# Token-major output projections, norms and residual stream with transposes back to feature-major

## The chip, the cores and the metric

The kernel runs on one core of one Trainium2 chip. A core has TensorE (PE: matmuls into PSUM), ScalarE (ACT), VectorE (DVE), GpSimd (POOL), SyncE (SP, which here issues most DMAs) and 16 DMA engines. The metric is device time in microseconds. The time before is 2262.39 us, the median of 3 runs (2261.51 to 2263.01).

## What is computed

Two layers of a diffusion backbone over 512 latent tokens and 256 context tokens, 1024 features, fp32. Layer 0 mixes tokens by retention (4 heads), layer 1 by HGRN2 (8 heads); each is followed by a gated convolutional FFN with 2816 hidden features. Cut to what the change touches:

```
mod = silu(c) @ ada_w[i] + ada_b[i]          # shift, scale, gate for each of two halves of a layer
u_l = rms_norm(h_l, norm_g[i, 0]) * (1.0 + sc1_l) + sh1_l
y_c, y_l = mixer(u_c, u_l, ...)              # ends in  (...) @ w_out
h_l = h_l + g1_l * rms_norm(y_l, norm_g[i, 1])
u_l = rms_norm(h_l, norm_g[i, 2]) * (1.0 + sc2_l) + sh2_l
h_l = h_l + g2_l * rms_norm(conv_ffn(u_l, ..., w_down), norm_g[i, 3])
# the same for the context stream with c_ctx, in layer 0 alone
```

The RMS norms go over the 1024 features of a token. The gain of a norm of y is the gate g times norm_g, one number per feature and per stream (latent or context).

## The kernel before

Activations lie feature-major: 128 features on the partitions, tokens along the free dimension, 8 feature tiles. Each matmul in fp32 precision is three in fp32r: every operand is split into a rounded part hi and a rest lo (`split`, L55: ScalarE writes hi, VectorE or GpSimd lo), and hi x hi, hi x lo, lo x hi are summed in PSUM. `weights` (L67) loads a weight block by a DMA on SP and splits it; raw, hi and lo have two buffers each. PSUM has six banks for large results (`acc`, L43) and two for small ones (`sml`, L46).

The order of PE's instructions is that of the program (`run`, L1200, puts PE under a manual schedule). The other engines' queues are ordered by the scheduler from a model of the timeline, except ScalarE in a part of `tail` (L444) and in the first stage.

The stages are `retention` (L582), `ffn` of layer 0 (L874), `hgrn` (L970) and `ffn` of layer 1, each ending in `tail` (L396), which also starts the next one. The output projection is done in parts while the stage still runs: for retention three heads of four (L844 to L858), for the FFN 18 of 22 hidden tiles in `down` (L919), for HGRN four heads of eight in `out1` (L1137). In these, weights are the stationary operand and tokens stream: one output tile is 128 features by 512 latent tokens and, in layer 0, 128 features by 256 context tokens. `evac` (L387) puts the sum into y in SBUF, by a copy on ScalarE the first time and by an add on VectorE after that.

`tail` does the last four k tiles in chunks of 256 tokens (three chunks with context, else two), 8 feature tiles each, 12 matmuls of 256 columns per tile (L401). For every chunk a generator `post` (L299) then does: load the residual h of the chunk by a DMA, squares of y on ScalarE and their pairwise sums on VectorE, the gain on ScalarE (L331), the sum over features by matmuls with a matrix of ones (`colsum`, L92, fp32), the root (`rstd`, L96: one on ScalarE, three refining steps on VectorE, each 256 wide on all partitions), the multiplication of y (L340, VectorE), the residual add (L343, mostly GpSimd), the store of h (L348, GpSimd's queue), the same norm for h, the multiplication (L355), modulation by A and B (`modulate`, L383, GpSimd) and the split into u (L368). `tail` calls the generators in pieces between the matmuls, and `lead` (L462) does the first four output tiles of the next stage, chunk by chunk, with the rest of the generators as hooks. In the last tail each quarter of a chunk is stored to the output (L345).

The modulation vectors come from `ada` (L200): pieces of work that fillers run between other matmuls; `finish` (L231) puts a section into feature-major form by a matmul with a selection table, and `modvec` (L276) multiplies it with the norm's weight.

Of the kernel before, what the change touches and what calls it, by code (L numbers as in the profile page):

```python
# [32 lines left out]
class Net:  # L33
# [70 lines left out]
    def setup(self):  # L104
        nc, cp = self.nc, self.cp
        cT = self.const("cT", eng=nc.sync)
        self.fold, self.ada_b, self.norm_g, self.sel = (self.const(c) for c in ("fold", "ada_b", "norm_g", "sel"))
        self.ones = cp.tile([P, P], F32, name="ones")
# [9 lines left out]
        self.mv = {}  # L118
        self.fill, self.acc_due, self.fin_due = deque(), None, None
# [80 lines left out]
    def ada(self, i, s, spread=False):  # L200
# [30 lines left out]
        def finish():  # L231
            n = 16 if spread else 64
            g = self.cp.tile([64, P], F32, tag="arow", name=f"arow{i}_{s}")[:n]
            nc.scalar.dma_start(g, scr.rearrange("j v (f c) -> (j v f) c", c=P))
            pt = self.sml(f"adat{i}_{s}", 16)
# [40 lines left out]
    def modvec(self, i, which):  # L276
# [3 lines left out]
        j, s = {"A1": (0, 1), "G1": (1, 2), "A2": (2, 4), "G2": (3, 5)}[which]  # L280
        gb = self.norm_g[:, i, j].unsqueeze(2).broadcast_to([P, NF, 2])
        o = self.cp.tile([P, NF, 2], F32, name=f"mv{i}{which}")
        if which[0] == "A":
            nc.vector.scalar_tensor_tensor(o, m[:, s], 1.0, gb, ALU.add, ALU.mult)
        else:
            nc.vector.tensor_tensor(o, m[:, s], gb, ALU.mult)
# [12 lines left out]
    def post(self, nm, chunk, y, hsrc, G, mods, u, hdst, big, tmp, early=False, fast=False, late=None):  # L299
# [4 lines left out]

        def squares(parts, kind):
            for p, a in enumerate(parts):
                q = pair(sums, p // 2) if p % 2 == 0 else tmp(f"q{kind}{p}{nm}").rearrange("p (a t) -> p a t", a=2)
                nc.scalar.activation(q, a, AF.Square)  # L308
                if p % 2:
                    nc.vector.tensor_tensor(pair(sums, p // 2), pair(sums, p // 2), q, ALU.add)  # L310

        def norm(kind):
            ps = self.sml(f"nps{kind}{nm}", W)
            if y is None:
                nc.vector.tensor_tensor(pair(sums, 0), pair(sums, 0), pair(sums, 1), ALU.add)
            self.colsum(ps, [sums[:, j] for j in range(2 if y is None else 4)])
            r = tmp(f"r{kind}{nm}")
            return self.rstd(r[:, :W], r[:, W:], ps, D)

        hx = big([P, NF + 4, W], F32, "hc" + nm)  # L320
        if early:
            yield "new"
# [3 lines left out]
        if y is not None:  # L326
# [19 lines left out]
            if u is None:  # L346
                return
# [957 lines left out]
```

## Time and profile before

| | |
|---|---|
| median of 3 runs | 2262.39 us (2261.51 to 2263.01) |
| the profiled execution's own time | 2261.59 us |
| its span in the profile | 2259.9 us |
| mean granted clock | 0.979 |
| PE busy | 2149.8 us (95%), 13144 matmuls |
| VectorE, ScalarE, GpSimd busy | 1403.3, 835.0, 429.5 us |
| DMA | 215.09 MB, mean 95 GB/s |

How to read it: a line of the page's groups gives the kernel line, engine, operation, the tiles written and read, shapes and count, then busy time and mean ns of one, then idle time of the engine before these instructions and what ended it. A row of a tile gives minimum, median and maximum duration, and the first and last start. In rows of time, the first number is the start in us from the span's start, the second how long the merged instructions took. The granted clock is that of TensorE, 1.00 being full speed. Matmuls are pipelined, so the duration of one is longer than the distance to the next.

### The profile page before, as it was taken

The numbers are of one execution on the slowest core, as the hardware profiler recorded it, in microseconds if no ns is written. First come the engines' busy times: TensorE is split into PE (matmuls) and PEld (weight loads), VectorE is DVE, ScalarE is ACT, GpSimd is POOL, SyncE is SP. The second block draws the span as 40 slices with busy tenths as digits, with TensorE's granted clock in tenths as the row PEclk, the third lists the DMA queues.
The fourth block names the chain that finished last, engine by engine and source line by source line (L and its number), as shares of the span: only waits on it lengthen the run. The fifth ranks groups of instructions, "written<-read, shape, count | busy, mean of one in ns | idle before, by whom it ended". The sixth has DMA issues, their size and how long they took to land. (4 is left out here: it accounts for less than half of the span.)

```text
span 2259.9 us, 32506 instructions
## 1 busy us (share of the span) xinstructions
PE 2149.8 (95%) x13144; PEld 1843.6 (82%) x13144; DVE 1403.3 (62%) x2546; ACT 835.0 (37%) x1575; POOL 429.5 (19%) x481
## 2 busy tenths in 40 slices
PE   7999999999899799999999979999999889999997
PEld 5888888888788788888888878888888668888886
DVE  6866675744515667467676577677777756434445
ACT  5542433423424333322132254434443444333323
POOL 4522130400102500000000055333333231000001
PEclk9999999999999899999999989999999999999998
DMA  8123213133123133333333422111111242232341
GB/s 284 57 67 124 81 57 125 53 122 113 56 73 119 63 112 104 122 112 117 108 112 127 154 75 85 57 39 57 39 57 42 91 150 87 92 104 94 102 135 43
DMA packets 204822, 215.09 MB, mean 95 GB/s; under 512 B 5760, under 2 KB 192512, under 8 KB 203904
## 3 DMA queue, kind: packets, MB, share of 16 engines
q1 hardware_dynamic: 199968, 198.90, 27.4%
q0 software_dynamic: 2608, 13.11, 1.7%
q8 instruction: 103, 1.69, 0.3%
q10 hardware_dynamic: 2096, 1.01, 0.2%
q14 instruction: 47, 0.39, 0.1%
HBM read 197.69 MB, written 15.31 MB: 94 GB/s over the span
## 5 line engine op out<-in xcount | busy, mean ns | idle before, releaser
L84 PE MATMUL f<-um,hua 128*128 128x512 f32 (+1 forms) x960 | 257.9, 356 | 0.0
L84 PE MATMUL f<-um,huv 128*128 128x512 f32 (+1 forms) x960 | 255.8, 354 | 0.0
L219 DVE SCALAR_TENSOR_TENSOR rows<-rada,sc,rows 128x256 f32<-128x256 f32 x504 | 232.2, 485 | 5.2
L84 PE MATMUL f<-gt,hd 128*128 128x512 f32 (+1 forms) x864 | 233.1, 358 | 0.0
L343 POOL TENSOR_TENSOR hce<-hce,yf 128x512 f32<-128x512 f32 x16 | 24.7, 1567 | 904.7 <-PE tl L407 538.5
L84 PEld LDWEIGHTS f<-um,hua 128*128 128x128 f32 x960 | 169.7, 189 | 28.5 <-issue 3.2
L84 PE MATMUL hp<-ue,hhw 128*128 128x512 f32 (+1 forms) x672 | 192.1, 373 | 0.0
L84 PEld LDWEIGHTS f<-um,huv 128*128 128x128 f32 x960 | 170.1, 189 | 25.2
L84 PEld LDWEIGHTS f<-gt,hd 128*128 128x128 f32 x864 | 152.4, 188 | 26.8 <-issue 0.6
L84 PE MATMUL f<-um,lua 128*128 128x512 f32 (+1 forms) x480 | 170.1, 354 | 0.0
L84 PE MATMUL f<-um,luv 128*128 128x512 f32 (+1 forms) x480 | 169.7, 354 | 0.0
L84 PE MATMUL f<-gt,ld 128*128 128x512 f32 (+1 forms) x432 | 154.4, 357 | 0.0
L84 PEld LDWEIGHTS hp<-ue,hhw 128*128 128x128 f32 x672 | 111.9, 189 | 17.7 <-issue 1.4
L676 PE MATMUL v<-hv,ua 128*128 128x512 f32 x384 | 120.5, 390 | 0.0
L84 PE MATMUL hp<-ue,lhw 128*128 128x512 f32 (+1 forms) x336 | 120.0, 357 | 0.0
L84 PEld LDWEIGHTS f<-um,lua 128*128 128x128 f32 x480 | 90.7, 189 | 13.0
L84 PEld LDWEIGHTS f<-um,luv 128*128 128x128 f32 x480 | 90.7, 189 | 12.6
L904 DVE TENSOR_TENSOR c<-f,c 128x512 f32<-128x512 f32 (+1 forms) x60 | 36.1, 601 | 100.7 <-PE f L84 100.6
L84 PEld LDWEIGHTS f<-gt,ld 128*128 128x128 f32 x432 | 81.2, 188 | 13.2
L891 ACT ACTIVATE c<-f,c_conv_b,c_conv_w 128x512 f32<-128x512 f32 (+1 forms) x60 | 41.9, 702 | 118.1 <-PE f L84 118.1
L84 PE MATMUL ld<-um,hfl 128*128 128x256 f32 x320 | 69.2, 313 | 17.1 <-ACT um L56 10.0
L1072 POOL TENSOR_SCALAR L<-Q 128x256 f32<-128x256 f32 x112 | 54.9, 505 | 160.9 <-PE hl L1085 63.0
(388 smaller groups left out, 5215.7 us busy)
## 6 DMA issues: line engine op xcount, KB each, us to landing
rada<-ada_w SPq DMA_DIRECT2D x48, 1024.0 KB
rua<-ffn_w_up SPq DMA_DIRECT2D x20, 1024.0 KB
ruv<-ffn_w_up SPq DMA_DIRECT2D x20, 1024.0 KB
rd<-ffn_w_down SPq DMA_DIRECT2D x24, 768.0 KB
rhw<-hg_w_in SPq DMA_DIRECT2D x32, 512.0 KB
rv<-ret_w_in SPq DMA_DIRECT2D x8, 1024.0 KB
rg<-ret_w_in SPq DMA_DIRECT2D x8, 1024.0 KB
rqk<-ret_w_in SPq DMA_DIRECT2D x6, 1024.0 KB
```

The lines of the kernel that those rows point to most:

```text
L84: nc.tensor.matmul(o, a, b[:, s], start=(i == 0), stop=(i == n - 1))
L219: nc.vector.scalar_tensor_tensor(rows[:, v], raw[:, k], a, rows[:, v], ALU.mult, ALU.add)
L343: eng.tensor_tensor(pair(hc, p), pair(hc, p), pair(y[p // 2][:, :, cs], p % 2), ALU.add)
L676: nc.tensor.matmul(ps, a, b, start=(c == 0 and k == 0 and z == 0), stop=(c == 1 and k == 3 and z == 2))
L891: nc.scalar.activation(c[:, s], ps, AF.Identity, bias=cb[:, i, mt : mt + 1], scale=w(1))
L904: nc.vector.tensor_tensor(c[:, s], ps, c[:, s], ALU.mult)
L1072: nc.gpsimd.tensor_scalar(vw(L[:, 1])[:, :, hf[1 - d]], vw(Q[:, d])[:, :, hf[1 - d]], 1.0, 0.0, ALU.mult, ALU.add)
```

## The change

The projections turn round: activations are now the stationary operand and the weights stream, so that an output tile is 128 tokens by 512 features; y and h lie token-major in blocks of 128 tokens (six blocks with context, four without). Each norm's sum over features is then along the free dimension and comes from the squares' accumulator output on ScalarE; the root and its refining steps work on one column. The gain, which is now along the free dimension, is a table of rows in DRAM (`gain_rows`), broadcast to all partitions by a DMA on ScalarE's queue. Once a block's unit-norm h is there, eight PE transposes of 128 x 128 bring it back to feature-major in PSUM, and ScalarE applies modulation while it evicts them, one feature tile at a time; the splits into u follow. GpSimd keeps only the stores of h and the lo part of some weights. `post` stays, as `norm_in`, for the first stage alone. The inputs gain a token-major copy of h and small tables; the output is token-major.

In the tail two column halves of a block follow one another; `n0` pairs run their first three k tiles ahead of the last. Transposes of the first blocks come between matmuls of the tail, the others as hooks in the lead. The weights of the projection loops are loaded in blocks of 512 columns (retention: six loads of 4 k tiles; down: four loads per part, of 3 k tiles). The DMA scratch of GpSimd's queue is set to 4096.

```diff
+    def gain_rows(self, i, s, g, n):
+        nc = self.nc
+        tab = self.cp.tile([16, 2, P], F32, tag="gtab", name=f"gtab{i}_{s}")
+        nc.scalar.dma_start(tab, self.t["gain_tab"][i, s // 5])
+        ps = self.sml(f"adag{i}_{s}", P)[0:16]
+        nc.tensor.matmul(ps, self.rsel[:n], g, start=True, stop=True)
+        nc.vector.tensor_tensor(tab[:, 0], ps, tab[:, 0], ALU.add)
+        nc.vector.scalar_tensor_tensor(tab[:, 0], tab[:, 0], -0.5 / D, tab[:, 1], ALU.mult, ALU.mult)
+        nc.scalar.dma_start(self.gains[i, s].rearrange("v (f c) -> (v f) c", c=P), tab[:, 0])
...
+    def handover(self, nm, y, hsrc, gain, mods, u, hdst, nb, big, tmp):
+        nc = self.nc
+        per = y[0].shape[1]
+        hx = [big([P, 3, D], F32, f"hx{nm}{j}") for j in range((nb + 2) // 3)]
+        if nb % 3:
+            g = hx[-1][:, 2:3]
+        else:
+            g = big([P, 3, D], F32, "gr" + nm)[:, 0:2]
+        small = lambda n, w: self.cp.tile([P, w], F32, tag=f"sm{w}", name=f"{n}{nm}", bufs=6)
+
+        def load():
+            rows = hsrc.rearrange("(b p) d -> p b d", p=P)
+            for j, x in enumerate(hx):
+                n = min(3, nb - 3 * j)
+                nc.sync.dma_start(x[:, :n], rows[:, 3 * j : 3 * j + n])
+            for v in range(g.shape[1]):
+                nc.scalar.dma_start(g[:, v], self.gains[gain][v : v + 1].broadcast_to([P, D]))
+
+        def block(b):
+            ts, v = slice(b * P, b * P + P), int(b >= 4)
+            yb, hb = y[b // per][:, b % per], hx[b // 3][:, b % 3]
+            ss = small(f"ss{b}", 4)
+            r = small(f"r{b}", 2)
+            for c in range(2):
+                cs = slice(c * 512, c * 512 + 512)
+                ps = yield
+                nc.vector.tensor_tensor(yb[:, cs], ps, yb[:, cs], ALU.add)
+                nc.scalar.activation(tmp(f"sq{nm}{b}{c}"), yb[:, cs], AF.Square, accum_out=ss[:, c : c + 1])
+            nc.vector.tensor_tensor(ss[:, 2:3], ss[:, 0:1], ss[:, 1:2], ALU.add)
+            ry = self.rstd(r[:, 0:1], r[:, 1:2], ss[:, 2:3], D)
+            nc.vector.scalar_tensor_tensor(yb, yb, ry, g[:, v], ALU.mult, ALU.mult)
+            nc.vector.tensor_tensor(hb, hb, yb, ALU.add)
+            if u is None:
+                nc.sync.dma_start(hdst[ts], hb)
+                yield "end"
+                return
+            nc.gpsimd.dma_start(hdst[ts], hb)
+            nc.scalar.activation(yb, hb, AF.Square, accum_out=ss[:, 3:4])
+            r2 = small(f"q{b}", 2)
+            rh = self.rstd(r2[:, 0:1], r2[:, 1:2], ss[:, 3:4], D)
+            nc.scalar.activation(yb, hb, AF.Copy, scale=rh)
+            yield "z"
+            A, B = mods()
+            z = yb.rearrange("p (f c) -> p f c", c=P)
+            for j in range(2):
+                ps = self.sml(f"tr{nm}{b}{j}")
+                for f in range(4):
+                    nc.tensor.transpose(ps[:, f * P : f * P + P], z[:, 4 * j + f], self.ident)
+                for f in range(4):
+                    k = 4 * j + f
+                    nc.scalar.activation(z[:, k], ps[:, f * P : f * P + P], AF.Identity,
+                                         scale=A[:, k, v : v + 1], bias=B[:, k, v : v + 1])
+                self.split(u[j][:, :, ts], u[2 + j][:, :, ts], z[:, 4 * j : 4 * j + 4])
+            yield "u"
+
+        return load, [block(b) for b in range(nb)]
 
...
+    def evac(self, y, b, c, ps, first):
+        per = y[0].shape[1]
+        dst = y[b // per][:, b % per, c * 512 : c * 512 + 512]
+        if first:
+            self.nc.scalar.activation(dst, ps, AF.Copy)
+        else:
+            self.nc.vector.tensor_tensor(dst, ps, dst, ALU.add)
+
+    def tail(self, w, x, y, nb, mk, nxt, mid=None):
+        load, gens = mk(nb)
+        load()
+        for g in gens:
+            next(g)
+
+        def part(b, c, kr, ps):
             for k in kr:
+                xh, xl = (z[:, b * P : b * P + P] for z in x(k))
+                for z, (l, r) in enumerate(((xh, w[c][0]), (xh, w[c][1]), (xl, w[c][0]))):
+                    self.nc.tensor.matmul(ps, l, r[:, k], start=(k == 0 and z == 0), stop=(k == 3 and z == 2))
+            if kr[-1] == 3:
+                gens[b].send(ps)
+
+        order = [(b, c) for b in range(nb - 2) for c in range(2)] + [(nb - 2 + b, c) for c in range(2) for b in range(2)]
+        n0 = 2 if mid is None else 4
+        pss = [self.acc(f"tl{self.uid()}") for _ in range(n0)]
+        for e, ps in zip(order, pss):
+            part(*e, range(3), ps)
+        if mid is not None:
+            self.filler(mid)
+        for e, ps in zip(order, pss):
+            part(*e, range(3, 4), ps)
+        done = 0
+        for n, (b, c) in enumerate(order[n0:], n0):
+            part(b, c, range(4), self.acc(f"tl{self.uid()}"))
+            if nxt and n >= 6 and n % 2 == 0 and done < nb - 3:
+                next(gens[done])
+                done += 1
         if not nxt:
             return None
         load, ctx = nxt[0]()
+        ws = [z() for z in load]
+        turn = lambda b: lambda: next(gens[b])
+        if nb == 6:
+            hooks = {(0, 0): turn(3), (0, 2): turn(4), (1, 0): turn(5)}
+        else:
+            turn(1)()
+            hooks = {(0, 0): turn(2), (0, 1): turn(3)}
+        return self.lead(ws, ctx, nxt[1](), BOTH if nb == 6 else LATENT, hooks)
 
...
-        y = [big([P, 4, T], F32, f"yr{j}") for j in range(2)]
-        for f0, f1 in ((0, 3), (3, 6), (6, 8)):
-            outs = [[(self.acc(f"wol{f}"), LAT), (self.acc(f"woc{f}", TC), CTX)] for f in range(f0, f1)]
+        y = [big([P, 3, D], F32, f"yr{j}") for j in range(2)]
+        for c in range(2):
+            outs = [self.acc(f"wo{c}{b}") for b in range(6)]
             for h in range(3):
-                wh, wl = self.weights(wo[:, 4 * h : 4 * h + 4, f0 * P : f1 * P], 4, (f1 - f0) * P, f"wo{f0}{h}")
-                for m in range(f1 - f0):
-                    ms = slice(m * P, m * P + P)
-                    for o, s in outs[m]:
-                        for k in range(4):
-                            for z, (a, b) in enumerate(((wh, 0), (wh, 1), (wl, 0))):
-                                nc.tensor.matmul(o, a[:, k, ms], ogs[h][b][:, k, s],
-                                                 start=(h == 0 and k == 0 and z == 0),
-                                                 stop=(h == 2 and k == 3 and z == 2))
-                self.filler(1)
-            for m in range(f1 - f0):
-                self.evac(y, f0 + m, outs[m], True)
+                wh, wl = self.weights(wo[:, 4 * h : 4 * h + 4, c * 512 : c * 512 + 512], 4, 512, f"wo{c}{h}")
+                for b, ps in enumerate(outs):
+                    for k in range(4):
+                        xh, xl = (ogs[h][z][:, k, b * P : b * P + P] for z in range(2))
+                        for z, (l, r) in enumerate(((xh, wh), (xh, wl), (xl, wh))):
+                            nc.tensor.matmul(ps, l, r[:, k], start=(h == 0 and k == 0 and z == 0),
+                                             stop=(h == 2 and k == 3 and z == 2))
+                    if h == 2:
+                        self.evac(y, b, c, ps, True)
+                self.filler(1 + (h == 1))
...
-                y.extend(big([P, 4, T], F32, f"yf{i}{j}") for j in range(2))
+                y.extend(big([P, nb // 2, D], F32, f"yf{i}{j}") for j in range(2))
             k0, nt = sum(sizes[:part]), sizes[part]
-            for c in range(4):
-                wh, wl = self.weights(wd[:, k0 : k0 + nt, c * 256 : c * 256 + 256], nt, 256, f"d{i}{part}{c}")
-                for m in range(2):
-                    ms = slice(m * P, m * P + P)
-                    outs = banks()
-                    self.mm3(outs, [(wh[:, k, ms], wl[:, k, ms], *gview(k, part)) for k in range(nt)])
-                    self.evac(y, 2 * c + m, outs, part == 0)
-                self.filler(c % 2)
+            for c in range(2):
+                outs = [self.acc(f"f{self.uid()}") for _ in range(nb)]
+                for k1 in range(0, nt, 3):
+                    wh, wl = self.weights(wd[:, k0 + k1 : k0 + k1 + 3, c * 512 : c * 512 + 512], 3, 512,
+                                          f"d{i}{part}{c}{k1}")
+                    for b, ps in enumerate(outs):
+                        for k in range(3):
+                            xh, xl = (z[:, b * P : b * P + P] for z in gview(k1 + k, part))
+                            for z, (l, r) in enumerate(((xh, wh), (xh, wl), (xl, wh))):
+                                nc.tensor.matmul(ps, l, r[:, k], start=(k1 + k == 0 and z == 0),
+                                                 stop=(k1 + k == nt - 1 and z == 2))
+                        if k1 + 3 == nt:
+                            self.evac(y, b, c, ps, part == 0)
+                self.filler(1)
 
...
-                    outs = [(self.acc(f"hwo{c}{m}"), LAT)]
+                    ps = self.acc(f"hwo{c}{m}")
                     ms = slice(m * P, m * P + P)
-                    yield from self.mm3g(outs, [(wh[:, k, ms], wl[:, k, ms], gh[0][:, k], gh[2][:, k]) for k in range(4)])
-                    self.evac(y, 4 * c + m, outs, True)
+                    yield from self.mm3g([(ps, ALL)], [(gh[0][:, k, ms], gh[2][:, k, ms], wh[:, k], wl[:, k]) for k in range(4)])
+                    self.evac(y, m, c, ps, True)
...
```

More of the change, by code (lines that the diff above doesn't have):

```diff
@@ L118, in setup @@
         self.mv = {}
+        self.gains = {k: self.dp.tile([2, D], F32, name=f"gain{k[0]}{k[1]}") for k in ((0, 2), (0, 5), (1, 2), (1, 5))}
         self.fill, self.acc_due, self.fin_due = deque(), None, None
@@ L303, in post @@
         pair = lambda x, p: x[:, 2 * p : 2 * p + 2]
[L305 to L318, printed above, removed]
         hx = big([P, NF + 4, W], F32, "hc" + nm)
-        if early:
-            yield "new"
+        yield "new"
         hc, sums = hx[:, :NF], hx[:, NF:]
@@ L349, in post @@
-        squares([pair(hc, p) for p in range(4)], "h")
-        yield "sq_h"
-        rb = norm("h").unsqueeze(1).broadcast_to([P, 2, W])
+        for p in range(4):
+            q = pair(sums, p // 2) if p % 2 == 0 else tmp(f"qh{p}{nm}").rearrange("p (a t) -> p a t", a=2)
+            nc.scalar.activation(q, pair(hc, p), AF.Square)
+            if p % 2:
+                nc.vector.tensor_tensor(pair(sums, p // 2), pair(sums, p // 2), q, ALU.add)
+        yield "sq_h"
+        ps = self.sml(f"npsh{nm}", W)
@@ L352, in post @@
+        nc.vector.tensor_tensor(pair(sums, 0), pair(sums, 0), pair(sums, 1), ALU.add)
+        self.colsum(ps, [sums[:, j] for j in range(2)])
+        r = tmp(f"rh{nm}")
+        rb = self.rstd(r[:, :W], r[:, W:], ps, D).unsqueeze(1).broadcast_to([P, 2, W])
         yield "norm_h"
-        z = [pair(hc, p) if y is None else pair(y[p // 2], p % 2)[:, :, cs] for p in range(4)]
         for p in range(4):
-            (nc.gpsimd if y is None and p > 1 else nc.vector).tensor_tensor(z[p], pair(hc, p), rb, ALU.mult)
+            (nc.gpsimd if p > 1 else nc.vector).tensor_tensor(pair(hc, p), pair(hc, p), rb, ALU.mult)
@@ L370, in post @@
-        if B is None:
-            for p in range(4):
-                self.modulate(pair(hc, p), pair(A, p), pair(late(), p), v)
-                self.split(*(pair(u[j + p // 2][:, :, cs], p % 2) for j in (0, 2)), pair(hc, p))
-            yield "late"
+            for f in range(2):
+                x, a = hc[:, 2 * p + f], A[:, 2 * p + f, v : v + 1]
+                nc.scalar.activation(uu[0][:, f], x, AF.Copy, scale=a)
+                nc.vector.scalar_tensor_tensor(uu[1][:, f], x, a, uu[0][:, f].bitcast(F32), ALU.mult, ALU.subtract)
@@ L877, in ffn @@
         wd = t["ffn_w_down"][i].rearrange("(k p) n -> p k n", p=P)
-        both = len(chunks) == 3
+        both = nb == 6
         width = T if both else TL
@@ L1204, in body, with joint @@
         t = self.t
[L1205 to L1207 removed]
+        self.h = self.dp.tile([T, D], F32, name="h_dram")
+        def joint(nm, gain, nxt, hsrc, hdst):
             st = []
```

170 lines of the change are left out of this document (39 added, 131 removed).

## The prediction

> **What bounds the kernel now.** I read the page first, then the windows by stage, then the rows of the tiles that the change touches, then single rows for prices.
>
> ```profile
> span 2259.9 us, 32506 instructions
> ...
> PE 2149.8 (95%) x13144; PEld 1843.6 (82%) x13144; DVE 1403.3 (62%) x2546; ACT 835.0 (37%) x1575; POOL 429.5 (19%) x481
> ...
> PE   7999999999899799999999979999999889999997
> ...
> PEclk9999999999999899999999989999999999999998
> ```
>
> TensorE is busy for 95% of the span, so only two things shorten it: less for PE to stream, or fewer of the holes. The holes are not spread out. They show in slices 1, 11, 14, 24, 32, 33 and 40; 14, 24 and 33 are the hand-overs between stages, where a tail (last part of an output projection, then norms and residual) meets the lead (first matmuls of the next stage). One hand-over in stretches of 5 us (stretch; then PE, PEld, DVE, ACT, POOL busy; granted clock; DMA share; GB/s):
>
> ```profile
> 730.00:735.00 5.00, 1.69 (x15) 1.48 (x13) 4.97 (x10) 1.83 (x4) 5.00 (x6) 1.00 0.59 196
> 735.00:740.00 5.00, 2.04 (x7) 1.54 (x7) 5.00 (x10) 3.34 (x7) 5.00 (x4) 0.57 0.04 14
> 740.00:745.00 5.00, 3.75 (x17) 3.70 (x17) 3.52 (x4) 1.42 (x3) 5.00 (x4) 0.50 0.63 213
> 745.00:750.00 5.00, 0.49 (x3) 0.25 (x2) 2.68 (x4) 3.36 (x7) 3.65 (x3) 0.84 0.09 34
> ```
>
> GpSimd is full while PE waits: the residual add and the modulation run there and VectorE's multiplications beside it. After each hole the granted clock falls to about 0.50, so a wait is paid again in slow matmuls. The tile rows give the length of each hand-over (the tail writes tl, the lead writes ld; first and last start):
>
> ```profile
> L407 PE MATMUL tl<-og,hwot x192: 277/283/469, 689.8 to 731.3; 128*128 128x256 f32 x192
> L84 PE MATMUL ld<-um,hfl x192: 278/283/583, 735.3 to 795.7; 128*128 128x256 f32 x192
> L407 PE MATMUL tl<-gt,hdt x192: 277/281/468, 1296.9 to 1338.1; 128*128 128x256 f32 x192
> L84 PE MATMUL ld<-ue,hhw x160: 274/283/582, 1342.1 to 1397.3; 128*128 128x256 f32 x160
> L407 PE MATMUL tl<-hgs,hhwt x128: 280/283/683, 1820.1 to 1846.2; 128*128 128x256 f32 x128
> L84 PE MATMUL ld<-um,hfl x128: 278/283/775, 1860.4 to 1897.7; 128*128 128x256 f32 x128
> L407 PE MATMUL tl<-gt,hdt x128: 277/281/468, 2217.0 to 2241.2; 128*128 128x256 f32 x128
> ```
>
> So the first takes 795.7 - 689.8 = 105.9 us, the second 100.4, the third 77.6 (together 283.9), and from the last tail to the end of the span 2259.9 - 2217.0 = 42.9 us. Each row is two thirds of its matmuls (hi weights; lo is the rest): 288 + 288, 288 + 240, 192 + 192 and 192.
>
> **Part by part. Streaming.** The pitch of matmuls in a full stream, from starts six instructions apart:
>
> ```profile
> 952.03 0.39 PE L84 MATMUL f<-um,lua 128*128 128x512 f32 x1
> ...
> 953.40 0.39 PE L84 MATMUL f<-um,lua 128*128 128x512 f32 x1
> 957.66 0.28 PE L84 MATMUL f<-um,lua 128*128 128x256 f32 x1
> ...
> 958.38 0.28 PE L84 MATMUL f<-um,lua 128*128 128x256 f32 x1
> ```
>
> A 512-wide one takes 1.37 / 6 = 0.228 us, a 256-wide one 0.72 / 6 = 0.120. Two narrow ones cost 0.240, so each pair that becomes one wide matmul saves 0.012. Outside the tails that is retention's output (288 narrow) and the first FFN's down (432 narrow): 360 pairs, 4.3 us, all on PE's full stretches. HGRN's and the second FFN's are 512 wide already. The new loops hold six PSUM banks over a pass; at 2.05 us for the 9 matmuls of a block, the last banks are needed 8 us after the first, and an eviction takes 0.69 (below), so I charge nothing. If one were late, it would cost that 0.69 per pass.
>
> **Norm sums go, transposes come.** The norms' sums over features are PE matmuls with ones:
>
> ```profile
> L94 PE MATMUL npshm<-hcm,ones 128*128 128x256 f32 x40 | 13.3, 475 | 8.4 <-DVE hcm L310 8.2
> L94 PE MATMUL npsye<-hce,ones 128*128 128x256 f32 x40 | 11.6, 436 | 8.8 <-DVE hce L310 8.8
> L94 PE MATMUL npsym<-hcm,ones 128*128 128x256 f32 x40 | 11.1, 428 | 4.5 <-DVE hcm L310 4.5
> L94 PE MATMUL npshe<-hce,ones 128*128 128x256 f32 x24 | 6.1, 390 | 1.6 <-DVE hce L310 1.5
> ...
> 2234.24 1.73 PE npsye L94 x8
> ...
> 1827.07 1.07 PE L171 MATMUL ada<-rada,sc 128*32 128x256 f32 x16
> ```
>
> Eight take 1.73 us, 0.216 each; 144 of them are 31.1 us (10.4, 10.4, 6.9, 3.5 by hand-over). In their place 16 blocks get 8 transposes each, 128 in all. HGRN has such transposes:
>
> ```profile
> 1439.38 0.60 PE L1101 MATMUL ht<-c_ident,AK 128*128 128x128 f32 x4
> 1439.74 0.72 PE L84 MATMUL hp<-ue,hhw 128*128 128x512 f32 x2
> ...
> L1101 PE MATMUL ht<-c_ident,AK 128*128 128x128 f32 x80 | 13.9, 273 | 0.0
> ```
>
> Four delay the next matmul by 0.36 us, 0.09 each; busy time by count is 13.9 / 80 = 0.174; one alone lasts 0.273. I take 0.12, nearer to the pitch since eight run in a row: 15.4 us.
>
> **Floors.** What PE must stream: first hand-over 144 x 0.228 + 48 x 0.12 + 288 x 0.12 = 73.2 us; second (240 in the lead) 67.4; third 96 x 0.228 + 32 x 0.12 + 192 x 0.12 + 1.1 for the modulation matmuls between (the L171 row) = 49.9. Before, the same sums with narrow tails and norm sums are 79.5, 73.8 and 54.1, so 26.4, 26.6 and 23.5 us were waits and slow clock.
>
> **Does the new chain keep up?** Now a block of 128 tokens is normed as soon as its two column halves are done, on ScalarE and VectorE; GpSimd loses its adds and modulations.
>
> ```profile
> 735.13 2.17 ACT L56 ACTIVATE hfl<-rfl 128x512 fp32r<-128x512 f32 x4
> L56 ACT ACTIVATE hfl<-rfl 128x512 fp32r<-128x512 f32 x16 | 8.7, 617 | 2.8 <-PE tl L407 2.8
> L891 ACT ACTIVATE c<-f,c_conv_b,c_conv_w 128x512 f32<-128x512 f32 x40 | 30.9, 772 | 91.1 <-PE f L84 91.1
> L891 ACT ACTIVATE c<-f,c_conv_b,c_conv_w 128x256 f32<-128x256 f32 x20 | 11.2, 561 | 27.0 <-PE f L84 26.9
> L686 ACT ACTIVATION_READ_ACCUMULATOR vr<-v 128x1 f32 x24 | 4.6, 194 | 0.0
> L394 DVE TENSOR_TENSOR yf<-f,yf 128x512 f32<-128x512 f32 x32 | 22.1, 689 | 55.5 <-PE f L84 55.2
> L687 DVE TENSOR_SCALAR vs<-vs 128x1 f32<-128x1 f32 x24 | 3.6, 152 | 42.4 <-ACT vr L686 42.4
> ```
>
> ScalarE in a row: (2.17 - 0.62) / 3 = 0.52 per 512 columns, so 1.04 for 1024; a summed square adds 0.19, and I price the one-column root at 0.19 too. With scale and bias, 512 and 256 columns cost 0.772 and 0.561, so 128 cost about 0.455, or 0.36 in a row (0.10 overlaps, as at 0.62 against 0.52). Per block: norm 2 x 0.71 + 1.23 + 1.04 + 2 x 0.19 = 4.1; after the transposes 8 x 0.36 + 2 x 0.52 = 3.9; together 8.0 us. VectorE per block: two evictions and two lo parts at 0.69, two 1024-wide at 1.38, seven one-column at 0.15: 6.6 us. ScalarE is the tighter one. The Trainium skill ("ScalarE: Activation LUTs", What ACT_TABLE_LOAD costs) speaks against splitting work into 128-wide activations: a fixed 186 ns each and 93 more per pointer operand, 93 overlapped, which by an estimate from that page makes 0.386 instead of 0.36 in a row, 0.2 us per block and 3 us over all blocks.
>
> First hand-over, from its start: blocks end every 5.5 us (24 x 0.228), the norm needs 4.1 of ScalarE. Up to the lead (PE there at 32.8 + 2.9 = 35.7) ScalarE must do four norms, a square, two blocks after transposition and 2.2 of weights: 27.1 us from about 4 on, done near 32 if nothing blocks. The lead's second chunk (PE at 49.1) needs another 17.5, near 50; the last (PE at 62.5) another 7.8, near 58. So it just fits, with no slack at the second chunk. Every block passes some ten times between ScalarE and VectorE, so I add 6 us of waits and slow clock to the first two hand-overs: 79 and 73. The third has four blocks, of which two end together at 9 + 4 x 0.68 = 11.9; ScalarE needs two norms, one more, two transposed blocks and 2.2 before the lead, 22.3 us from about 10 on, so the lead starts near 32 where PE is there at 24.8: 58 with that wait. What could also be late there is GpSimd's lo part of the first lead weights, which must wait until a tail weight's buffer is free (after group 10 of 12, 27.4 us in):
>
> ```profile
> L57 POOL TENSOR_TENSOR lfl<-rfl,hfl 128x512 fp32r<-128x512 f32 x8 | 12.9, 1640 | 5.2 <-ACT hfl L56 5.2
> ```
>
> 27.4 + 0.6 + 4 x 1.64 = 34.6 us, just under 35.7; GpSimd also issues the blocks' stores, and one of them that waits ahead of these four would push the lead. Loads of h in longer rows and the gains (two rows broadcast, 1 MB, on ACT's queue) replace equal loads on SP; at the 196 to 213 GB/s of the windows above 1 MB takes 5 us, before the 8 us at which the first block wants it. Free; without cover 5 us once. The gain rows' small matmuls replace small ones: nothing. Sum of the hand-overs: 283.9 - (79 + 73 + 58) = 73.9.
>
> **The end.**
>
> ```profile
> 2253.41 1.67 DVE hce L343
> 2255.08 0.60 DVEq L1301
> ```
>
> The chain ends on the final store, 2259.9 - 2255.08 = 4.8 us after the last add. New: 96 x 0.228 = 21.9, then eviction 0.69, square 0.71, sum and root 0.34, three small 0.45, two 1024-wide 2.76 (about 5.5 with hops), a block of 512 KB instead of 256 in the last store (5 to 6): 34 with 0.7 behind the block before. 42.9 - 34 = 8.9 saved (6 to 11).
>
> Total 4.3 + 73.9 + 8.9 = 87.1 us from the profiled execution's 2261.59: 2174.5. The median of the runs is 0.8 above that execution, too little to matter: I say **2174**.
>
> **Rivals.** (a) Nothing waits: the floors hold, 283.9 - 190.5 = 93.4, the end gives 11: 2153. For: VectorE and ScalarE both fit by the sum. Against: in-order queues and no slack. (b) ScalarE and VectorE alternate rather than overlap, a block costing 11 us: first hand-over 4.1 + 66 + 4.4 weights + 11.5 (last chunk) = 86, second 80, third 9.9 + 44 + 4.4 + 11.5 = 70; 26 more than forecast: 2201. (c) Transposes don't overlap: 128 x (0.273 - 0.12) = 20 more: 2194.
>
> ```profile
> 1808.00:1809.00 1.00, 1.00 (x14) 0.57 (x6) 0.00 (x0) 0.42 (x2) 0.00 (x0) 1.00 0.00 0
> ```
>
> Against it: transposes ran in this microsecond at granted clock 1.00. The Trainium skill ("TensorE: Matmul & The Clock Gate", Part 4: PE-mode transpose) gives about 275 ns in a kernel and says that they don't count as busy for the full clock; the duration agrees with 273, the pitch of 0.09 and the clock do not. (d) The waits aren't the chain's but what both kernels keep (lead weights, loads): the old 76.5 us come back on the floors, and the end keeps its length: 2261.6 - 16.9 - 4.3 = 2240. (e) Slower: blocks run one after another, VectorE's queue held by one block's adds while ScalarE waits, and the lead's last chunks run at the clock of 0.50 seen behind holes. With x us per block and the lead's last chunk at half speed (third: 23) the three take 88.9 + 16 x; equal to before, with 13.2 saved elsewhere, at x = 13.0. At 14: 2277. Against: work of different blocks is independent and 8.0 is far from 13.
>
> **How the numbers follow.** Forecast 0.57, (a) 0.15, (b) 0.17, (c) 0.04, (d) 0.03, (e) 0.04. The range takes in (a) with 7 us for cheaper transposes and (b) with 7 for longer waits: 2146 to 2208; some 0.15 lie outside. About 4.5 us (0.2%) is what a measurement can tell from no change. Faster is all but (e) and a sliver of (d): 0.95, same 0.01, slower 0.04.
>
> **What would show it.** Rows of tl: 128x512, a third as many instructions as tl and its norm sums had. No npsy, npsh but the first stage's. Transposes 128 more, near 0.12 in a row. From tl's first to ld's last start 79, 73, 58 us; granted clock in these windows mostly 1.00; GpSimd's share far below 19%; ScalarE near full in them. If ld waits on ACT u tiles for over 5 us per chunk, (b) is right; on POOL's lo weights or a DMA, (d). Full FFN stretches must stay at 5.00 of 5 us, or the six-bank loops cost something that I set at nothing.

## The result and the profile after

The changed kernel takes **2201.34 us** (median of 4 runs, 2200.28 to 2201.90) beside 2262.28 us for the kernel before in the same session: the ratio is 0.973, with a 95% interval from 0.9713 to 0.9747. So 61 us are saved where 87 were forecast. The profiled execution took 2201.44 us, its span 2199.7.

The page of the kernel after (span; busy time and share by engine; TensorE's busy tenths and granted clock in 40 slices):

```profile
span 2199.7 us, 30760 instructions
...
PE 2113.7 (96%) x12288; PEld 1779.3 (81%) x12288; DVE 1340.3 (61%) x2500; ACT 864.3 (39%) x1695; POOL 323.0 (15%) x395
...
PE   7999999999899899999999999999999879999998
...
PEclk9999999999999999999999999999999999999999
```

GpSimd has fallen from 19% to 15%, and no slice is below 9 in the clock row any more. In TensorE's row the 7 of slice 24 is gone, slices 14 and 40 are 8 instead of 7; slice 33, with the third hand-over in it, is 7 where it was 8. The lengths come from the tile rows, as before. First the tails (tl) of the first two hand-overs and the end, then the leads (ld):

```profile
L435 PE MATMUL tl<-hwot,og x96: 388/389/628, 687.2 to 727.8; 128*128 128x512 f32 x96
L435 PE MATMUL tl<-hdt,gt x96: 388/396/628, 1274.1 to 1315.0; 128*128 128x512 f32 x96
L435 PE MATMUL tl<-hhwt,hgs x64: 387/389/792, 1776.4 to 1807.8; 128*128 128x512 f32 x64
L435 PE MATMUL tl<-hdt,gt x64: 388/394/397, 2167.1 to 2189.3; 128*128 128x512 f32 x64
...
L84 PE MATMUL ld<-um,hfl x192: 274/283/562, 728.0 to 773.4; 128*128 128x256 f32 x192
L84 PE MATMUL ld<-ue,hhw x160: 278/283/562, 1315.2 to 1352.4; 128*128 128x256 f32 x160
L84 PE MATMUL ld<-um,hfl x128: 280/283/582, 1818.0 to 1846.6; 128*128 128x256 f32 x128
```

The tails are 512 wide, as the change says. Read as in the prediction, from the first start of tl to the last of ld:

| stretch, us | before | forecast | after |
|---|---|---|---|
| start to first tail | 689.8 | 688.1 | 687.2 |
| first hand-over | 105.9 | 79 | 86.2 |
| first FFN | 501.2 | 498.6 | 500.7 |
| second hand-over | 100.4 | 73 | 78.3 |
| HGRN | 422.8 | 422.8 | 424.0 |
| third hand-over | 77.6 | 58 | 70.2 |
| second FFN | 319.3 | 319.3 | 320.5 |
| last tail to the end | 42.9 | 34 | 32.6 |

The hand-overs keep 44.2 us above the forecast's floors (234.7 against 190.5). TensorE's longest waits in them (what waited, for what, us in all, times, longest; the rows left out between belong to other stages) show where most of that is:

```profile
PE trm L396 <- ACT yh L389: 12.0, 3, 5.6
PE trm L396 <- ACT yr L389: 9.0, 3, 4.0
...
PE tre L396 <- ACT yf L389: 7.1, 4, 3.1
...
PE ld L84 <- ACT um L56: 2.7, 1, 2.7
```

Four rows make 30.8 us. All but the last are waits at L396, the PE transposes, for L389, the copy on ScalarE that leaves a block with unit norm. The matmuls of tail and lead that stand behind the transposes in TensorE's order have to wait with them. The windows of the first hand-over (columns as in the prediction) show the rest:

```profile
705.00:710.00 5.00, 5.00 (x28) 4.23 (x27) 4.06 (x11) 4.50 (x14) 0.53 (x1) 1.00 0.26 105
...
715.00:720.00 5.00, 4.13 (x19) 3.08 (x17) 2.64 (x9) 5.00 (x16) 0.43 (x1) 1.00 0.01 2
720.00:725.00 5.00, 2.26 (x12) 2.03 (x13) 4.96 (x4) 3.82 (x8) 5.00 (x4) 0.89 0.00 0
725.00:730.00 5.00, 5.00 (x26) 4.28 (x26) 2.64 (x3) 4.08 (x12) 2.55 (x2) 0.77 0.30 57
730.00:735.00 5.00, 1.03 (x9) 0.83 (x7) 4.91 (x13) 4.98 (x11) 0.00 (x0) 0.92 0.70 258
735.00:740.00 5.00, 4.97 (x23) 4.97 (x24) 2.60 (x5) 3.75 (x10) 0.53 (x1) 0.50 0.54 162
```

From 705 to 740 ScalarE is at 3.75 to 5.00 of 5 us, VectorE nearly fills two of the windows, and behind the two holes of TensorE of 3.6 and 4.0 us comes a low clock (0.77, 0.50), the same picture as before with shorter holes. Behind the hole of 1.4 us ahead of the sixth block's transposes the clock stays at 1.00 (windows from 750 to 760).

### The profile page after: what moved, and what is told of

Same layout as the page of the kernel before. It is cut to its first block, busy times and chain, and to the rows that moved or that the text cites. A ratio compares the mean times of both kernels' runs of the same rounds, so it can differ in the third digit from the quotient of the medians.

```text
span 2199.7 us, 30760 instructions
## 1 busy us (share of the span) xinstructions
PE 2113.7 (96%) x12288; PEld 1779.3 (81%) x12288; DVE 1340.3 (61%) x2500; ACT 864.3 (39%) x1695; POOL 323.0 (15%) x395
## 5 line engine op out<-in xcount | busy, mean ns | idle before, releaser
L937 PE MATMUL f<-hd,gt 128*128 128x512 f32 x720 | 228.2, 396 | 0.0
L937 PEld LDWEIGHTS f<-hd,gt 128*128 128x128 f32 x720 | 134.9, 187 | 33.6 <-issue 0.8
L937 PE MATMUL f<-ld,gt 128*128 128x512 f32 x360 | 142.2, 395 | 0.0
L860 PE MATMUL wo<-hwo,ogr 128*128 128x512 f32 x288 | 89.4, 391 | 1.9 <-ACT ogr L56 1.6
L57 DVE TENSOR_TENSOR lua<-rua,hua 128x512 fp32r<-128x512 f32 x80 | 50.5, 685 | 57.4 <-ACT hua L56 57.2
L56 ACT ACTIVATE hua<-rua 128x512 fp32r<-128x512 f32 x80 | 44.2, 620 | 103.6 <-DMA rua<-ffn_w_up 51.9
```

Source lines behind the costliest of these rows:

```text
L56: self.nc.scalar.activation(hi, raw, AF.Copy)
L57: (eng or self.nc.vector).tensor_tensor(lo, raw, hi.bitcast(F32), ALU.subtract)
L860: nc.tensor.matmul(ps, l, r[:, k], start=(h == 0 and k == 0 and z == 0), stop=(h == 2 and k == 3 and z == 2))
L937: nc.tensor.matmul(ps, l, r[:, k], start=(k1 + k == 0 and z == 0), stop=(k1 + k == nt - 1 and z == 2))
```

## The experiments

Three theories stood against one another. **ORDER**: the transposes stand too early in TensorE's program, and ready matmuls wait behind them. **THROUGHPUT**: ScalarE has too much to do per block. **ALTERNATION** (rival (b) of the prediction): a block passes between ScalarE and VectorE so often that its steps add up. **CONTENTION** (GpSimd's work slows VectorE's) was a smaller suspect, and alignment a question beside it. All times are medians of 4 runs (10 for before_align); hand-overs are read as above. The scheduler orders the queues of ScalarE and VectorE anew for each kernel, so a run below can differ from the changed kernel in that too.

| kernel | us | first, second, third hand-over |
|---|---|---|
| after | 2201.3 | 86.2, 78.3, 70.2 |
| late | 2202.9 | 85.8, 80.6, 71.0 |
| lovec | 2197.5 | 84.5, 78.9, 67.5 |
| evict2 | 2228.0 | 91.3, 88.2, 80.7 |
| align | 2193.8 | 85.1, 78.1, 70.2 |
| diag | 2199.9 | 82.4, 77.7, 72.2 |
| evsplit | 2187.5 | 79.3, 73.9, 67.0 |
| turn2 | 2201.7 | 84.8, 78.6, 70.4 |
| combo | 2179.1 | 79.8, 74.1, 66.8 |
| newton | 2193.0 | 83.4, 77.7, 66.1 |
| best | 2179.7 | 79.7, 74.2, 66.9 |
| best_late | 2170.3 | 77.3, 71.7, 63.8 |

### late: the transposes later in TensorE's order

```diff
-            if nxt and n >= 6 and n % 2 == 0 and done < nb - 3:
+            if nxt and nb == 6 and n >= 8 and n % 2 == 0 and done < 2:
...
-            hooks = {(0, 0): turn(3), (0, 2): turn(4), (1, 0): turn(5)}
+            hooks = {(0, 0): turn(2), (0, 2): turn(3), (1, 0): turn(4), (1, 1): turn(5)}
...
+            turn(0)()
             turn(1)()
-            hooks = {(0, 0): turn(2), (0, 1): turn(3)}
+            hooks = {(0, 1): turn(2), (0, 2): turn(3)}
```

> Every block's transposes stand one or two output tiles (5 to 6 us) later in TensorE's order; nothing else is changed. In the changed kernel TensorE waits 28 us in all, nearly all of it at the transposes, for the unit-norm copy on ScalarE (L389), with finished work for other tiles queued behind. Theory ORDER (the transposes are asked for too early, and the waits are the latency of one block's chain): most of these waits go, some 15 to 20 us fall away, 2181 to 2187 us, and the first weight product of the next stage waits no more than 3 us per hand-over for u. Theory THROUGHPUT (ScalarE and VectorE need longer per block than TensorE's tiles, as rival (b) of the prediction has it): the waits only move to the matmuls that read u, 2198 to 2205 us.

Measured 2202.9 us, no gain. Its waits of TensorE:

```profile
PE ld L84 <- ACT um L56: 12.5, 4, 7.0
PE trm L396 <- ACT yh L389: 11.8, 2, 8.8
...
PE ld L84 <- ACT ue L56: 8.1, 2, 6.9
```

The waits of the first two hand-overs left the transposes and stand at the lead's first matmuls, which want u; that is 32.4 us in three rows, against 30.8 in four. (The second row shown is the third hand-over, whose waits stayed at the transposes.) ORDER falls as the explanation of the changed kernel: the blocks are late, and where TensorE meets them matters little.

### lovec: the low part of the lead's weights on VectorE

```diff
-            return self.weights(wu[:, :, c : c + 256], NF, 256, f"fl{i}{c}", None if c else self.nc.gpsimd)
+            return self.weights(wu[:, :, c : c + 256], NF, 256, f"fl{i}{c}")
...
-        return [lambda: self.hgrn_w(0, 1, 2, self.nc.gpsimd), lambda: self.hgrn_w(0, 0, 4)], (True, False)
+        return [lambda: self.hgrn_w(0, 1, 2), lambda: self.hgrn_w(0, 0, 4)], (True, False)
```

> The subtraction that makes the low part of the next stage's first weights runs on VectorE instead of GpSimd; nothing is left out. Theory CONTENTION (GpSimd's four operations of 1.2 to 1.9 us slow VectorE's chain, 1.07 instead of 0.16 us for one column and 2.28 instead of 1.28 for 1024, just when blocks 2 and 3 are wanted): the chain is some 4 us shorter and four VectorE operations of 0.7 us come in, so 2 to 4 us less per hand-over, 2189 to 2196 us. Theories ORDER and THROUGHPUT of ScalarE give no gain: 2199 to 2205 us.

Measured 2197.5 us, 3.8 less. What CONTENTION saw is in the order of time of the kernel after (start, us, engine, line):

```profile
719.57 7.46 POOL L57 TENSOR_TENSOR lfl<-rfl,hfl 128x512 fp32r<-128x512 f32 x4 [8.03 <-ACT hfl L56]
719.77 1.07 DVE L101 SCALAR_TENSOR_TENSOR r3m<-r3m 128x1 f32<-128x1 f32 x1
721.37 2.28 DVE L379 SCALAR_TENSOR_TENSOR yr<-yr,r3m,grm 128x1024 f32<-128x1024 f32 x1
723.69 2.19 DVE L380 TENSOR_TENSOR hxm<-hxm,yr 128x1024 f32<-128x1024 f32 x1
```

The same instructions of VectorE in lovec:

```profile
720.50 0.15 DVE L101 SCALAR_TENSOR_TENSOR r3m<-r3m 128x1 f32<-128x1 f32 x1
721.77 1.28 DVE L379 SCALAR_TENSOR_TENSOR yr<-yr,r3m,grm 128x1024 f32<-128x1024 f32 x1
724.77 1.22 DVE L380 TENSOR_TENSOR hxm<-hxm,yr 128x1024 f32<-128x1024 f32 x1
```

While GpSimd subtracts, these three operations of VectorE take about 1 us more each (1.07, 2.28, 2.19 against 0.15, 1.28, 1.22); without it they are normal. Not every one is slowed: a split at 720.77, with two inputs in SBUF as well, took its usual 0.68 us. In the third hand-over a single column on the way to an awaited copy took 2.55 us (at 1798.76), in lovec 0.16. The Trainium skill ("SBUF — State Buffer", Who interferes with whom) says that a VectorE instruction with two inputs in SBUF contends with a GpSimd instruction that reads SBUF; these are such, and the trace agrees for them. The contention is real and shown, but its removal is worth only 4 of the 44 us, with the twelve subtractions that VectorE now does itself set against it.

### evict2 and evsplit: ScalarE's load

```diff
-                    nc.scalar.activation(z[:, k], ps[:, f * P : f * P + P], AF.Identity,
-                                         scale=A[:, k, v : v + 1], bias=B[:, k, v : v + 1])
+                    for _ in range(2):
+                        nc.scalar.activation(z[:, k], ps[:, f * P : f * P + P], AF.Identity,
+                                             scale=A[:, k, v : v + 1], bias=B[:, k, v : v + 1])
```

> Each of the eight evictions behind a block's transposes is issued twice (the second writes the same values): 8 x 0.36 = 2.9 us more of ScalarE for each of 16 blocks, 46 us in all. Theory THROUGHPUT: nearly all of it comes on the time, 35 to 46 us, 2236 to 2247 us. Theory ORDER (ScalarE is busy 66 of 95 us around the first hand-over, so it has room): only the evictions that stand ahead of an awaited copy count, 10 to 20 us, 2211 to 2221 us.

Measured 2228.0 us, 26.7 more, between the two theories. ScalarE's busy time rose by 43 us (907.5 against 864.3), so 0.62 of it came on the time.

```diff
+                    if f % 2:
+                        nc.vector.tensor_scalar(z[:, k], ps[:, f * P : f * P + P], A[:, k, v : v + 1],
+                                                B[:, k, v : v + 1], ALU.mult, ALU.add)
+                    else:
...
```

> Every second eviction behind the transposes goes to VectorE (multiply and add with the same two operands per partition); nothing is left out. 16 x 4 x 0.36 = 23 us of ScalarE move to VectorE. Theory THROUGHPUT OF SCALARE: by the 0.58 that the doubled evictions showed, 13 us less, 2186 to 2190 us. Theory ALTERNATION, strictly taken (a block costs the sum of both engines): no change, 2199 to 2204 us. In between if both engines evict side by side but VectorE's own chain is then late: 2191 to 2197 us.

Measured 2187.5 us, 13.8 less, as THROUGHPUT has it. The groups of the evictions that VectorE took over and of those left on ScalarE, for the first hand-over:

```profile
L400 DVE TENSOR_SCALAR yr<-trm,mv0A,mod 128x128 f32<-128x128 f32 x24 | 9.2, 406 | 6.1 <-ACT yr L403 5.9
L403 ACT ACTIVATE yr<-trm,mod,mv0A 128x128 f32<-128x128 f32 x24 | 10.2, 450 | 6.5 <-PE trm L396 6.4
```

One costs about the same on either engine (9.2 / 24 = 0.38 us, 10.2 / 24 = 0.42), so 16 x 4 of them moved. ScalarE's busy time fell by 20.7 us (843.6 against 864.3), and 0.67 of that came off the time. Strict ALTERNATION falls: work moved from one engine to the other does help.

### newton: two steps of the block's chain fewer

```diff
+    def rstd1(self, r, ssum, n):
+        self.nc.scalar.activation(r, ssum, AF.Abs_reciprocal_sqrt, bias=self.eps, scale=1.0 / n)
+        self.nc.vector.tensor_scalar(r, r, -2.0 * n, None, ALU.mult)
+        return r
...
-            ry = self.rstd(r[:, 0:1], r[:, 1:2], ss[:, 2:3], D)
+            ry = self.rstd1(r[:, 0:1], ss[:, 2:3], D)
...
-            rh = self.rstd(r2[:, 0:1], r2[:, 1:2], ss[:, 3:4], D)
+            rh = self.rstd1(r2[:, 0:1], ss[:, 3:4], D)
```

> The hand-overs' roots lose their refining step: one operation of one column on VectorE instead of three, twice per block (what is left out is that refinement, so the values differ slightly). ScalarE's work is as in the changed kernel; the chain of a block is 2 x 2 x 0.19 = 0.76 us shorter. Theory THROUGHPUT OF SCALARE: no more than 2 us less, 2199 to 2202 us. Theory ALTERNATION (what a block takes is the sum of its steps, one after the other): 16 x 0.76 = 12 us less, 2189 us; half of that, 2195 us, would leave it between.

Measured 2193.0 us, 8.3 less, with ScalarE's work unchanged (864.0 us). That is 0.68 of the 12.2 us that by the estimate above left the chains, and it leaves THROUGHPUT of ScalarE alone unable to explain the result. Nor is it VectorE's load that counted: newton took 13.3 us from it (1327.0 against 1340.3), but evsplit put 16.5 on it (1356.8) and was faster still. Together with the two runs above: of each us taken from or added to a block's steps on ScalarE or VectorE, some two thirds show in the time. That fits steps that largely run one behind the other, with the other third covered by work of other blocks; the next two runs show that it is no rule for every step.

### diag and turn2: the turn itself

In diag the unit-norm copy is replaced by a diagonal in the turning matmul:

```diff
-            nc.scalar.activation(yb, hb, AF.Copy, scale=rh)
+            dg = self.cp.tile([P, P], F32, tag="dg", name=f"dg{nm}{b}", bufs=3)
+            nc.vector.tensor_scalar(dg, self.ident, rh, None, ALU.mult)
...
-                    nc.tensor.transpose(ps[:, f * P : f * P + P], z[:, 4 * j + f], self.ident)
+                    nc.tensor.matmul(ps[:, f * P : f * P + P], hb[:, (4 * j + f) * P : (4 * j + f + 1) * P], dg, start=True, stop=True)
```

> The unit-norm copy on ScalarE (L389, 1.04 to 1.14 us per block) goes: the residual rows themselves are turned, by a matmul with a diagonal of the row factors (the identity times the factor, 128 wide, on VectorE) in place of each PE transpose. Theory THROUGHPUT OF SCALARE: doubling the evictions put 26.7 us on the time for 46.4 us of ScalarE, 0.58 of it; 16 x 1.1 x 0.58 = 10 us less, 2189 to 2193 us. Theory ALTERNATION (ScalarE and VectorE work one after the other within a block, so that whatever leaves the chain of one block counts in full): 16 x (1.1 - 0.2) = 14 us, 2185 to 2189 us. Against both: the matmuls may take longer than the 0.11 us of a transpose; at twice that 14 us come back, 2200 us or more.

In turn2 each transpose is issued twice:

```diff
-                    nc.tensor.transpose(ps[:, f * P : f * P + P], z[:, 4 * j + f], self.ident)
+                    for _ in range(2):
+                        nc.tensor.transpose(ps[:, f * P : f * P + P], z[:, 4 * j + f], self.ident)
```

> Each of the 128 transposes is issued twice into the same place. The prediction priced one at 0.12 us in a row, and the trace after has eight in 1.03. Theory IN A ROW: 128 x 0.11 = 14 us at most, all of it where TensorE is on the chain of the block and 8 to 14 us in all, 2209 to 2216 us. Rival (c) of the prediction (a transpose costs its whole 0.273 us): 35 us, 2230 us or more. If TensorE's waits at the transposes hide them: below 5 us.

diag measured 2199.9 us, 1.4 less; turn2 2201.7, the same as after. The first block's turn in the kernel after, then in diag:

```profile
706.29 1.03 PE L396 MATMUL trm<-c_ident,yr 128*128 128x128 f32 x8
```

```profile
706.74 1.95 PE L397 MATMUL trm<-dgm,hxm 128*128 128x128 f32 x16
```

The matmul with the diagonal became two instructions each: sixteen in 1.95 us instead of eight in 1.03, so a block's turn is 0.92 us longer, about what the copy had cost. Yet turn2, whose turns are as long (1.91 us for the first block), lost nothing, though 0.88 us more for each of 16 blocks' turns make 14 us: a step on TensorE did not count as those on ScalarE and VectorE did. So rival (c) falls. Where diag's gain went is not settled: it took 17.6 us from ScalarE (846.7 against 864.3), of which two thirds would have been 12. After turn2 the longer turn alone is an unlikely reason; the diagonal's place in VectorE's queue, and the new order of the queues, are candidates that no run here separates.

### align: 32 bytes in the FFN's pool

```diff
         cw, cb = self.const("conv_w", pool=fp), self.const("conv_b", pool=fp)
+        nc.vector.memset(fp.tile([P, 8], F32, name=f"pad{i}"), 0.0)
```

> A pad of 32 bytes in the FFN's pool moves its tiles to a 64-byte boundary; the program's memory plan has gt at byte 111584 of a partition, 32 past one, and ogr, um, ua and hgs on one. The matmuls that read gt take 233.3 ns for 512 columns in both FFNs, the same matmuls from the other tiles 226.7. If the place is what costs the 6.6 ns: 1080 matmuls of the down projections and 240 of the two tails, 1320 x 6.6 ns = 8.7 us less, 2191 to 2194 us, their pitch 226.7. If it is something else about these matmuls (the weights of three blocks at a time, the order of the banks): 2200 to 2203 us, their pitch 233.3.

Measured 2193.8 us, 7.6 less. Stretches of the second FFN's chain, 144 matmuls of the down projection and 288 of up, in the kernel after:

```profile
1914.17 33.59 PE f L937 x144
1947.77 65.29 PE f L84 x288
```

and with the pad:

```profile
1909.63 32.64 PE f L938 x144
1942.27 65.28 PE f L84 x288
```

The up projection stays at 0.2267 us each; down goes from 33.59 / 144 = 0.2333 to 0.2267. The place of the tile in SBUF is what cost 6.6 ns per matmul. The first FFN is 4.2 us shorter, the second 2.9, the end 0.7.

The same pad in the kernel before:

> The kernel before with the pad of 32 bytes in the FFN's pool. Its matmuls with gt take 234 ns for 512 columns and 117 for 256, where others take 227 and 120, which is why two narrow ones cost as much as one wide one and the change saved nothing in the first FFN. If the pad brings both to 227 and 120: 864 wide x 6.6 = 5.7 us less, 912 narrow x 3 = 2.7 us more, 2259 us; the first FFN is then some 4 to 5 us longer than that of the changed kernel with the pad (496.4 us), about 500 to 501. If only the wide ones change: 2256 us. If the pad does nothing here, where gt is the moving operand: 2262 us.

Measured 2257.6 us (ratio to before 0.9984, interval 0.9974 to 0.9993), between the values for both kinds and for the wide ones alone. In its trace both moved: the wide matmuls on gt from 0.233 to 0.227 us each, the narrow ones from 0.118 to 0.120. The first FFN takes 500.1 us, the changed kernel with the pad 496.5: between aligned kernels the change saves 3.6 us there, where it saved 0.5 between the unaligned.

### combo, best and best_late: putting gains together

combo holds the edits of diag, evsplit, lovec and align; best leaves diag out; best_late adds the edit of late to best.

> Together: the diagonal instead of the copy, every second eviction on VectorE, the low parts of the lead's weights on VectorE, the pad for alignment. If the parts add up: 7.6 (align, measured) + 3.8 (low parts, measured) + 10 + 13 = 34 us less than 2201, 2167 us. Where they shorten the same waits or fill VectorE, less: 2168 to 2182 us. The floors of the three hand-overs leave 234.7 - 190.5 = 44 us at most, so not below 2149 us.

> Every second eviction on VectorE, the low parts of the lead's weights on VectorE, the pad; the unit-norm copy and the PE transposes as in the changed kernel. If the three measured gains add up (13.8 + 3.8 + 7.6 = 25 us): 2176 us, 3 less than with the diagonal, whose matmuls would then have cost more than the copy that they replace. If the first two shorten the same waits: up to 2180 us, as with the diagonal.

> The same as the run beside it, with every block's transposes one or two tiles later in TensorE's order, as tried before. Now that ScalarE has room: theory ORDER (what is left of the waits at the transposes, 13.7 us with the evictions split, is their place) gives 4 to 8 us less than the run beside it. Theory THROUGHPUT (the blocks' own pace) gives the same within 2 us, or more time, since the lead's first block is then ready later.

combo took 2179.1 us and best 2179.7: diag adds nothing, and evsplit with lovec gives 21.6 - 7.6 = 14.0 us beyond the pad, little more than evsplit's 13.8 alone, so these two seem to shorten the same waits. best_late took **2170.3 us**, 9.4 less than best and more than ORDER expected; the ratio to before is 0.960 (0.9584 to 0.9612). Its waits at the hand-overs:

```profile
PE trm L396 <- ACT yh L389: 7.0, 2, 6.5
...
PE ld L84 <- ACT um L56: 2.8, 1, 2.8
PE trm L396 <- DVE yr L400: 2.2, 1, 2.2
PE tre L396 <- DVE yf L400: 2.2, 1, 2.2
```

14.2 us instead of 30.8. The first two hand-overs are within 4.1 and 4.3 us of their floors (77.3 and 71.7 against 73.2 and 67.4), the third still 13.9 above. The edit that gave nothing to the changed kernel gives 9.4 once the blocks come faster: here TensorE's order was worth something only after the pace was better.

## Why the forecast was right in direction and too large

**The step that failed** is the third part's "ScalarE must do four norms, a square, two blocks after transposition and 2.2 of weights: 27.1 us from about 4 on, done near 32 if nothing blocks". The load was right in sum. The busy time of the engines from about the first square (692.93, 1280.03 and 1787.85; the windows of the second and third begin somewhat ahead of it) to the lead's first matmul, in the three hand-overs (DVE and ACT are the third and fourth):

```profile
692.93:728.00 35.07, 31.46 (x144) 25.86 (x143) 25.76 (x48) 28.44 (x68) 9.64 (x8) 0.95 0.28 105
1279.00:1315.20 36.20, 33.11 (x149) 26.66 (x148) 26.15 (x49) 28.37 (x68) 9.57 (x8) 0.95 0.19 68
1785.00:1817.90 32.90, 19.58 (x93) 15.18 (x92) 20.63 (x39) 22.56 (x56) 6.67 (x7) 0.87 0.44 153
```

ScalarE did 28.4 us in the first (27.1 forecast) and 22.6 in the third (22.3 forecast). But from its first square it needed 35.1 and 30.1 us for it, and it began 5.7 us after the tail's start in the first (692.93 - 687.2) and 11.5 in the third (1787.85 - 1776.4; 4 and 10 forecast). So the lead began 40.8 us in where TensorE could have been there at 35.7, and in the third hand-over 41.6 in where 32 was forecast. The first block shows what a norm takes (its two evictions by VectorE, the last steps to its copy, and its evictions behind the transposes):

```profile
692.21 1.37 DVE L375 TENSOR_TENSOR yr<-tl,yr 128x512 f32<-128x512 f32 x2 [1.13 <-PE tl L435]
...
698.35 1.23 DVE L380 TENSOR_TENSOR hxm<-hxm,yr 128x1024 f32<-128x1024 f32 x1
...
699.66 1.06 ACT L386 ACTIVATE yr<-hxm 128x1024 f32<-128x1024 f32 x1 [1.78 <-issue]
...
702.94 1.14 ACT L389 ACTIVATE yr<-hxm,q0m 128x1024 f32<-128x1024 f32 x1
...
707.46 1.49 ACT L399 ACTIVATE yr<-trm,mod,mv0A 128x128 f32<-128x128 f32 x4
```

With little of other blocks ahead of it, its norm takes from 692.2 to 704.1, 11.9 us, of which 4.1 were priced on ScalarE; in between ScalarE waits for VectorE and VectorE for ScalarE. A table load on ScalarE (ACT_TABLE_LOAD, 1.28 us at 694.36) is in it too, for which the sum had no term. TensorE does not wait for this block; in the first hand-over it waits for the third, the fourth and the sixth. The third (the last step of its second root on VectorE, a split of the lead's weights and the copy on ScalarE, the transposes):

```profile
717.43 0.16 DVE L101 SCALAR_TENSOR_TENSOR q2m<-q2m 128x1 f32<-128x1 f32 x1
...
718.80 2.24 ACT L56 ACTIVATE hfl<-rfl 128x512 fp32r<-128x512 f32 x4
...
721.49 1.19 ACT L389 ACTIVATE yr<-hxm,q2m 128x1024 f32<-128x1024 f32 x1
...
722.74 1.09 PE L396 MATMUL trm<-c_ident,yr 128*128 128x128 f32 x8 [3.61 <-ACT yr L389]
```

The root was ready at 717.59, but its copy began 3.9 us later: ScalarE did other work first, the split among it, and TensorE waited 3.61 us. The third block of the second hand-over is alike (3.5 us, a wait of 3.09), and 2.6 us of the 4.00 for the fourth block of the first. So by this reading some 9 of the 28 us at the transposes lie with the order of ScalarE's queue. The two longest waits, 5.6 and 5.1 us in the third hand-over, do not: there the copy began within 0.6 us of its root. No run changed that order alone, and what newton and evsplit gained cannot be kept wholly apart from it: in both, the third block's copy stands ahead of the split (717.80 and 719.36 in newton), and its wait is gone.

I had charged 6 us of waits per hand-over for the passages between the engines; the first two show 13.0 and 10.9 us above their floors, the third 20.3 where I had 8.

**Rival (b)** named the passing between the engines, and its numbers, 2201 us and 86, 80 and 70, are those measured. Its price was not: evictions of the first block start 20.3 us after the tail's start (707.46 - 687.2) and of the sixth at 753.33, so a block follows another after 9.2 us on average with the lead's weights among them, not 11. That the sums agree is luck: by (b) the sixth block is done 74.5 us in and 11.5 remain; here its u was complete at 758.07, 70.9 us in, and 15.3 remained to the lead's last matmul. The sign named for (b), ld waiting on u for over 5 us per chunk, did not show (2.7 us, once), since the transposes stand ahead and wait in its place. And in three runs two thirds of a change in the steps on ScalarE and VectorE came on the time, not all.

```profile
753.33 2.90 ACT L399 ACTIVATE yr<-trm,mod,mv0A 128x128 f32<-128x128 f32 x8 [0.81 <-PE trm L396]
```

That row also settles a price: 2.90 / 8 = 0.363 us per eviction in a row, as forecast from the rows of before (0.36). The estimate of 0.386 from the Trainium skill ("ScalarE: Activation LUTs", What ACT_TABLE_LOAD costs) was a little too dear; the trace decides.

**Streaming** was mis-sized: 0.5 us in the first FFN (2.6 forecast), because the pitch of 0.228 and 0.120 was read from matmuls on u and used for gt, whose tiles lie unaligned. before_align and align show the 2.6 and more to be there when they are aligned. The retention up to its tail gave 2.6 us (1.7 forecast), but the runs above differ there by 2 us, though they leave it alone (686.5 to 688.5). HGRN became 1.2 us longer, less than these runs differ there (422.6 to 425.6); the second FFN became 1.2 us longer too, and why was not tried.

**Transposes** cost 1.03 / 8 = 0.13 us each in a row (0.12 forecast), at granted clock 1.00 in the window of the first of them (705 to 710), and twice as many cost nothing; behind a long hole eight took 1.97 us (at 735.03, at a clock of 0.50). What the Trainium skill ("TensorE: Matmul & The Clock Gate", Part 4: PE-mode transpose) gives, about 275 ns, is the duration of one here as well (median 273), but not what one costs in a row. **GpSimd's low part** ended 39.8 us in (727.03 - 687.2) instead of 34.6, because it began 32.4 us in instead of 28.0 and took 7.46 / 4 = 1.87 us each instead of 1.64; lovec prices the whole matter at 3.8 us. The **end** is 32.6 us where 34 was forecast. **(a)**, **(d)** and **(e)** fall: waits are there, they follow the chain, and they are shorter than before.

What stays open: how much of the waits lies with the order of ScalarE's queue and how much with the chain itself, the third hand-over's last 13.9 us in best_late, and diag.

## What to carry to other kernels

When small blocks go back and forth between two in-order engines, price one block's whole chain, from its first input to its last output, before adding up either engine's load: an engine that fits by its sum may still stand idle for a fifth of the time (28.4 us of work in 35.1). Look also at what stands ahead of an awaited step in its engine's queue. Then shorten the chain first, and only then move the consumer's place in its own queue; in the other order the second edit showed nothing here. And read a stream's pitch from the very tiles that a change will stream, since the same matmul had two prices here.

## What the runs showed of the hardware

Matmuls of 512 columns that read a tile 32 bytes past a 64-byte boundary (by the program's memory plan) took 233.3 ns instead of 226.7, both as the stationary operand (after) and as the moving one (before: 233 ns); with 256 columns moving they took 118 ns instead of 120, less and not more. Moving the tile by 32 bytes gave 7.6 us in this kernel.

The fp32 matmul with the diagonal was issued as two instructions, a PE transpose as one (16 in 1.95 us against 8 in 1.03).
